# A decoder layer on one core: the order of three products at the opening of the mix

## The chip, the cores and the metric

The kernel runs on one core of a Trainium2 chip. The metric is the device time of one execution in microseconds (us); less is better. A core has five engines with a queue each: PE (matrix products, with its weight loads shown as PEld), DVE and POOL (elementwise work), ACT (elementwise functions and copies; it also issues DMAs) and SP (issues DMAs). Each engine takes the instructions of its queue in the order in which they were emitted.

## The reference

One layer of a hybrid decoder is computed for 1024 prompt tokens and 64 sample tokens (8 sequences of 8), 1088 in all, in float32:

```
h = x + 0.5 * swiglu(rmsnorm(x), ffn1)
n = rmsnorm(h)
proj = n @ w_in        # split into qkv_pre, z, a, b, q_s, k_s, v_s
qkv  = silu(causal_conv(qkv_pre))          # 12 tiles of 128 columns
g, beta = f(a), sigmoid(b)                 # a and b: 4 columns each, the "logits"
o_g  = gated_delta_chunked(qkv, g, beta)   # chunks of 64, a triangular solve per chunk, a state carried on
o_s  = sliding-window attention(q_s, k_s, v_s)
h = h + concat(o_g, o_s) @ w_out
h = h + 0.5 * swiglu(rmsnorm(h), ffn2)
h = h + sigmoid(rmsnorm(h) @ ple_gate) * (p @ ple_proj);  y = rmsnorm(h)
```

The middle part, from `n @ w_in` to the product with `w_out`, is called the mix.

## The kernel before, in words

Activations lie transposed, with 128 features on the partitions and the 1088 tokens along a row, and are worked on in four quarters of 272 columns (`QW`), numbered 0 to 3; quarters 0 and 1 are the first half, 2 and 3 the second. To keep float32 accuracy each operand is split into a high and a low part (`split`: ACT casts the high part, DVE or POOL subtracts to get the low one), and a product of one 128-column tile with one quarter is three products for each of 8 blocks of the inner dimension: 24 matmuls of 128x272, called a wide group here. In the trace they are `pm<-xn,t`.

The mix follows a hand-written list, `ORDER`: ('T', m) is the projection of tile m of `w_in`, ('co', m) its transposes back, ('sc',) the scalars from the logits, 'so' the triangular solves, 'lv' the levels that join solved blocks, 'pre', 'go' and 'out' the steps of the state, 'swa' the attention. A scheduler takes the program in this order and fixes each engine's queue, so that rows of neighbouring steps are interleaved on each engine.

The mix opens before the list is walked. Three products are cut into parts by quarter and their parts are collected in `joint`, by `logits()` and by `conv_in` for the first two tiles, 5 and 6:

- **the logits (L)**: 16 columns of weights for a and b. A group for one quarter is 16 matmuls, 8 with 16 and 8 with 8 columns of weights, on 272 columns (`pm<-xn,w`, form 16x272 and 8x272 in the order). The small weight tile w is loaded, cast on ACT and its low part taken on DVE (L207 `w<-raw,w`). Banks: pool g, two buffers.
- **tile 5 (A)**: four wide groups; those of quarters 0 and 1 go into one bank each of pools c and a, those of 2 and 3 into pool m, which has two buffers.
- **tile 6 (B)**: four wide groups, all in pool m.

All three use activations to which only the gain of the norm is applied; the root of each token is multiplied in when a group is evicted by DVE (`pre<-pm,r` for tiles, `abT<-pm,r` for the logits). For each half `mix_roots` forms the roots: sums on PE (`pss`), a chain of short DVE rows (`nv`, `nry`, `nrt`, `np`), diagonals on DVE and POOL (`dg`); `nm.sums` then spreads them with PE (`pb`) and copies them on ACT (`r<-pb`). No group of a half is evicted before that copy. The loop below counts the groups from n = 0 to 11, half by half: sums of the first half behind group 4, evictions from group 5 on, roots of the second half behind group 5, its sums behind group 7.

```
groups = [(half, part, 2 * half + i) for half in range(2) for part in parts_ for i in range(2)]
for n, (half, part, ci) in enumerate(groups):
    evs.append(part(ci))
    if n in (4, 7):
        nm.sums(half)
    if n >= 5 and n != 6:
        while evs:
            evs.pop(0)()
    if n == 5:
        mix_roots(1)
```

Behind the loop `lend()` transposes the logits (`pa<-ident,abT`) and stores them in `ab`. Then the list goes on: the short convolution of tile 5 (ACT L837, three DVE rows L839 over 1024 and three over 64 tokens, silu on ACT L840), its transposes (`ptk`), and the projection of the next tile, 4. The scalars (`ctmp`, `csg`) need `ab`; the decays of the chunks (`gu` on POOL, `pdc` on PE) need the scalars.

Of the kernel before, what the change touches and what calls it, by code (L numbers as in the profile page):

```python
# [150 lines left out]
def decoder_layer(ctx: ExitStack, tc: tile.TileContext, mix_off, a, o):  # L151
# [628 lines left out]
    joint = [None]  # L780
# [707 lines left out]
    ends = [conv_in(m, w) for m, w in zip(tiles[:2], ws)]  # L1488
    for e in ends:
        next(e)  # L1490
    parts_, joint[0] = joint[0], None
    def mix_roots(c):
        nm.roots(c, pt, "t", [B(b, [HW], "dg", F32R) for b in (14, 15)])

# [167 lines left out]
```

## Time and profile before

| | |
|---|---|
| median of three runs | 2326.74 us |
| the three runs | 2315.22, 2326.94, 2326.74 us |
| the profiled execution, its own time | 2301.93 us |
| its span, first to last instruction | 2300.1 us |
| PE busy in the span | 2234.6 us (97%) |
| DVE, ACT, POOL busy | 1424.9, 885.2, 528.8 us |
| mean granted clock of PE | 0.979 |

The profile is of one execution, which was 24.8 us shorter than the median of the three runs beside it; 1.8 us of its time lie outside the span. [...] Busy shares are means over stages: the first feed-forward part ends at about 768 us, the mix lies between there and about 1360 us, and the second feed-forward part and the gate fill the rest.

### The profile page before, as it was taken

The numbers are of one execution on the slowest core, as the hardware profiler recorded it, in microseconds if no ns is written. First come the engines' busy times: TensorE is split into PE (matmuls) and PEld (weight loads), VectorE is DVE, ScalarE is ACT, GpSimd is POOL, SyncE is SP. The second block draws the span as 40 slices with busy tenths as digits, with TensorE's granted clock in tenths as the row PEclk, the third lists the DMA queues.
The fourth block names the chain that finished last, engine by engine and source line by source line (L and its number), as shares of the span: only waits on it lengthen the run. The fifth ranks groups of instructions, "written<-read, shape, count | busy, mean of one in ns | idle before, by whom it ended". The sixth has DMA issues, their size and how long they took to land. (4 is left out here: it accounts for less than half of the span.)

```text
span 2300.1 us, 43650 instructions
## 1 busy us (share of the span) xinstructions
PE 2234.6 (97%) x17440; PEld 2181.6 (95%) x17440; DVE 1424.9 (62%) x2753; ACT 885.2 (38%) x1728; POOL 528.8 (23%) x448
## 2 busy tenths in 40 slices
PE   8999999999999999989999999999999999999997
PEld 8999999999999898889896789999999999999997
DVE  8866556975333477865654657866556684443667
ACT  6433333444322264322235654433333344332444
POOL 0043332210010334242321000333333210011324
PEclk9999999999999999988996999999999999999999
DMA  5322222367433245455552565222222258433234
GB/s 190 106 82 84 67 76 85 108 201 260 141 112 118 80 139 153 120 147 173 156 172 88 159 195 176 93 85 81 71 76 85 71 160 286 134 100 112 92 97 129
DMA packets 179354, 290.90 MB, mean 126 GB/s; under 512 B 33391, under 2 KB 87663, under 8 KB 179151
## 3 DMA queue, kind: packets, MB, share of 16 engines
q1 hardware_dynamic: 128288, 225.82, 32.2%
q10 hardware_dynamic: 50863, 62.29, 7.8%
q8 instruction: 137, 2.24, 0.4%
q14 instruction: 66, 0.54, 0.1%
HBM read 220.53 MB, written 66.83 MB: 125 GB/s over the span
## 5 line engine op out<-in xcount | busy, mean ns | idle before, releaser
L177 PE MATMUL pd<-xa,t 128*128 128x272 f32 x4224 | 531.8, 288 | 5.5 <-DVE s L463 3.8
L177 PEld LDWEIGHTS pd<-xa,t 128*128 128x128 f32 x4224 | 530.4, 188 | 6.8 <-DVE s L463 4.3
L177 PE MATMUL pm<-xn,t 128*128 128x272 f32 x2112 | 297.8, 297 | 15.0 <-DVE pre L824 7.2
L207 DVE TENSOR_TENSOR t<-raw,t 128x1024 fp32r<-128x1024 f32 x128 | 163.6, 1278 | 238.5 <-ACT t L206 235.8
L177 PEld LDWEIGHTS pm<-xn,t 128*128 128x128 f32 x2112 | 278.6, 194 | 21.3 <-DVE pre L824 8.5
L206 ACT CAST t<-raw 128x1024 fp32r<-128x1024 f32 x150 | 157.1, 1047 | 295.3 <-PE pd L177 226.8
L177 PE MATMUL pS<-lT,hS 128*128 128x272 f32 x900 | 260.4, 289 | 0.0
L177 PE MATMUL pS<-hT,lS 128*128 128x272 f32 x900 | 260.1, 289 | 0.0
L177 PE MATMUL pS<-hT,hS 128*128 128x272 f32 x900 | 259.1, 288 | 0.0
L207 DVE TENSOR_TENSOR lA<-raw,hA 128x512 fp32r<-128x512 f32 x171 | 136.9, 804 | 58.5 <-ACT hA L206 52.2
L177 PE MATMUL pA<-hB,lA 128*128 128x272 f32 x600 | 172.6, 288 | 0.0
L177 PE MATMUL pA<-hB,hA 128*128 128x272 f32 x600 | 172.5, 288 | 0.0
L177 PE MATMUL pA<-lB,hA 128*128 128x272 f32 x600 | 172.1, 287 | 0.0
L177 PEld LDWEIGHTS pS<-hT,hS 128*128 128x128 f32 x900 | 169.6, 188 | 0.0
L177 PEld LDWEIGHTS pS<-hT,lS 128*128 128x128 f32 x900 | 169.3, 188 | 0.0
L177 PEld LDWEIGHTS pS<-lT,hS 128*128 128x128 f32 x900 | 169.2, 188 | 0.0
L206 ACT CAST hA<-raw 128x512 fp32r<-128x512 f32 x171 | 105.8, 620 | 161.0 <-PE pA L177 121.6
L206 ACT CAST hS<-raw 128x512 fp32r<-128x512 f32 x145 | 89.4, 620 | 176.5 <-PE pS L177 154.2
L259 POOL TENSOR_TENSOR r<-r,sq 128x544 f32<-128x544 f32 x28 | 47.1, 1684 | 425.3 <-ACT sq L258 424.1
L207 DVE TENSOR_TENSOR lS<-raw,hS 128x512 fp32r<-128x512 f32 x145 | 127.8, 881 | 17.6 <-ACT hS L206 4.8
L463 DVE TENSOR_TENSOR u<-u,pS 128x272 f32<-128x272 f32 x225 | 91.1, 432 | 54.8 <-PE pS L177 54.6
L177 PEld LDWEIGHTS pA<-lB,hA 128*128 128x128 f32 x600 | 113.0, 188 | 0.0
(363 smaller groups left out, 4687.9 us busy)
## 6 DMA issues: line engine op xcount, KB each, us to landing
raw<-in_gu SPq DMA_DIRECT2D x114, 512.0 KB
raw<-in_dn SPq DMA_DIRECT2D x88, 512.0 KB
scrU<-act ACTq DMA_DIRECT2D x88, 272.0 KB
a<-scrU SPq DMA_DIRECT2D x88, 272.0 KB
raw<-in_gate SPq DMA_DIRECT2D x24, 512.0 KB
raw<-in_w_in SPq DMA_DIRECT2D x22, 512.0 KB
raw<-in_w_out SPq DMA_DIRECT2D x16, 512.0 KB
h<-in_x SPq DMA_DIRECT2D x2, 2176.0 KB
```

Source lines behind the costliest of these rows:

```text
L177: i = T.matmul(out, lhsT=lhsT, rhs=rhs, start=start, stop=stop)
L206: S.copy(hi, src)
L207: return eng.tensor_tensor(out=lo, in0=src, in1=hi.bitcast(F32), op=ALU.subtract)
L259: G.tensor_tensor(out=self.acc[c], in0=self.acc[c], in1=sq, op=ALU.add)
L463: i_ = V.tensor_tensor(out=I[c][out], in0=I[c][x], in1=pt_, op=ALU.add)
```

## The change

The list of collected parts is turned by one place, so that in each half the groups come as A, A, B, B, L, L in place of L, L, A, A, B, B. Nothing is computed otherwise; the numbers 4, 5, 6 and 7 in the loop stay, so the sums of the first half now stand behind the first logits group, those of the second behind tile 5's last group.

```
-    parts_, joint[0] = joint[0], None
+    parts_, joint[0] = joint[0][1:] + joint[0][:1], None
```

The queues are decided by the scheduler, which had already put wide groups ahead of the first logits. On PE at the opening, in the first half (`pss<-ones,r_6230` are the sums for its roots, `w_8999` is the weight tile of the logits; the logits' rows that follow alternate in the two forms):

```order
 L177 MATMUL pss<-ones,r_6230 128x2 x4
 L177 MATMUL pss<-ones,r_6230 32x2
-L177 MATMUL pm<-xn,t 128x272 x69
+L177 MATMUL pm<-xn,t 128x272 x96
 L177 MATMUL pm<-xn,w_8999 16x272
```

Before, 69 wide matmuls stood ahead of the first logits row (A's two groups and 21 rows of B's first); now 96 do, all four wide groups of the half. The numbers of rows in the opening are the same.

Further on, on DVE, in the convolution of tile 4 beside the projection of tile 7 (`pre<-pm,r_6230` are evictions of the projection, `cv` rows are the convolution):

```order
 L839 SCALAR_TENSOR_TENSOR cv<-pre,vecs,cv 128x1024
-L839 SCALAR_TENSOR_TENSOR cv<-pre,vecs,cv 128x64
 L824 TENSOR_TENSOR pre<-pm,r_6230 128x272
-L839 SCALAR_TENSOR_TENSOR cv<-pre,vecs,cv 128x1024
-L839 SCALAR_TENSOR_TENSOR cv<-pre,vecs,cv 128x64
-L839 SCALAR_TENSOR_TENSOR cv<-pre,vecs,cv 128x1024
+L839 SCALAR_TENSOR_TENSOR cv<-pre,vecs,cv 128x64
+L839 SCALAR_TENSOR_TENSOR cv<-pre,vecs,cv 128x1024
+L839 SCALAR_TENSOR_TENSOR cv<-pre,vecs,cv 128x64
 L824 TENSOR_TENSOR pre<-pm,r_6230 128x272
+L839 SCALAR_TENSOR_TENSOR cv<-pre,vecs,cv 128x1024
 L839 SCALAR_TENSOR_TENSOR cv<-pre,vecs,cv 128x64
```

Between the two evictions two long convolution rows stood before and one stands now.

In the levels, on DVE before (the first piece) and after (the second); `rot` is a tile that a DMA fills and POOL multiplies, `L1048` evicts the last product of the first two chunks:

```order
L1076 SCALAR_TENSOR_TENSOR X<-pkq,cssA,X 128x128 x4
L1030 TENSOR_TENSOR Pm<-plv,ctile 128x4x64 x3
L1048 TENSOR_SCALAR lv<-plv 64x4x64 x2
L1197 TENSOR_TENSOR xq<-xq,rope 128x1088
L1037 TENSOR_TENSOR lv<-lv,plv 128x8x32
```

```order
L1076 SCALAR_TENSOR_TENSOR X<-pkq,cssA,X 128x128 x4
L1030 TENSOR_TENSOR Pm<-plv,ctile 128x4x64 x3
L1197 TENSOR_TENSOR xq<-xq,rope 128x1088
L1048 TENSOR_SCALAR lv<-plv 64x4x64 x2
L1037 TENSOR_TENSOR lv<-lv,plv 128x8x32
```

The two evictions L1048 have moved behind the rotary row L1197; L1037 stands behind it in both.

In the attention, on ACT before (the first piece) and after (the second), behind the scaling of one attention unit (L1282); `sc<-px` copies transposed weights of the attention out of PSUM, `cvz` is the silu of a z tile:

```order
L1282 ACTIVATE sc<-sc,se 128x128 x2
L206 CAST t<-raw 128x1024
L1364 ACT_TABLE_LOAD
L1364 ACTIVATE cvz<-cvz 128x1088
L1287 COPY sc<-px 128x512
```

```order
L1282 ACTIVATE sc<-sc,se 128x128 x2
L1287 COPY sc<-px 128x2x128
L1287 COPY sc<-px 128x512
L206 CAST t<-raw 128x1024
L1262 ACTIVATE sc,den<-sc,nmx 128x256 x4
```

The copies have moved ahead of the cast, the table load and the silu.

## Rows read from the trace of the kernel before

**Rows 1.** The page: span, busy time of the engines.
```profile
span 2300.1 us, 43650 instructions
PE 2234.6 (97%) x17440; PEld 2181.6 (95%) x17440; DVE 1424.9 (62%) x2753; ACT 885.2 (38%) x1728; POOL 528.8 (23%) x448
```

**Rows 2.** Windows: stretch, length, busy time by engine, granted clock, DMA share, GB/s.
```profile
768.86:802.00 33.14, 30.02 (x233) 26.86 (x231) 18.72 (x56) 6.58 (x13) 11.55 (x14) 0.95 0.27 89
802.00:956.00 154.00, 148.39 (x1151) 143.78 (x1150) 116.31 (x252) 79.82 (x186) 58.65 (x68) 0.99 0.44 129
956.00:1013.00 57.00, 46.30 (x319) 45.14 (x318) 46.35 (x58) 15.96 (x47) 20.89 (x14) 0.88 0.59 159
1216.00:1248.00 32.00, 29.79 (x108) 21.02 (x109) 11.51 (x44) 16.77 (x49) 6.53 (x4) 0.52 0.40 132
1248.00:1300.00 52.00, 50.37 (x351) 36.66 (x352) 32.25 (x131) 33.79 (x113) 1.91 (x1) 0.93 0.39 119
```

**Rows 3.** Timeline of PE at the opening: start, length, row, [idle before, releaser].
```profile
768.86 8.91 PE L177 MATMUL pm<-xn,t 128*128 128x272 f32 x69
780.89 5.39 PE L177 MATMUL pm<-xn,w 128*16 128x272 f32 x32 [3.12 <-DVE w L207]
...
789.99 1.10 PE L177 MATMUL pss<-ones,r 128*128 128x2 f32 x10
791.02 4.13 PE L177 MATMUL pm<-xn,w 128*16 128x272 f32 x32
...
808.50 4.76 PE L177 MATMUL pm<-xn,t 128*128 128x272 f32 x36
```

**Rows 4.** Window around that idle time, columns as in rows 2.
```profile
780.00:784.00 4.00, 3.10 (x15) 1.94 (x16) 0.84 (x6) 0.06 (x1) 1.27 (x5) 0.57 0.92 298
```

**Rows 5.** Timeline of DVE at the opening.
```profile
780.66 0.18 DVE L207 TENSOR_TENSOR w<-raw,w 128x64 fp32r<-128x64 f32 x1
...
787.44 0.43 DVE L801 TENSOR_TENSOR abT<-pm,r 16x272 f32<-16x272 f32 x1 [6.60 <-ACT r L266]
```

**Rows 6.** Timeline of ACT at the opening.
```profile
783.94 0.21 ACT L892 ACTIVATE ctmp<-vecs 128x4 f32<-128x4 f32 x1 [4.37 <-POOL lmask L744]
786.95 0.68 ACT L266 COPY r<-pb 128x272 f32<-128x272 f32 x2 [2.81 <-PE pb L177]
```

**Rows 7.** Timelines of PE, DVE and POOL, and a window, 829 to 840 us.
```profile
829.15 3.25 PE L177 MATMUL pm<-xn,t 128*128 128x272 f32 x24
832.88 0.33 PE L177 MATMUL pdc<-gu,lmask 64*64 64x256 f32 x1 [0.48 <-POOL gu L948]
834.89 0.60 PE L177 MATMUL pm<-xn,t 128*128 128x272 f32 x1 [1.68 <-DVE pre L824]
...
829.01 3.35 DVE L839 SCALAR_TENSOR_TENSOR cv<-pre,vecs,cv 128x1024 f32<-128x1024 f32 x1
...
829.01 5.47 DVE L839 SCALAR_TENSOR_TENSOR cv<-pre,vecs,cv 128x1024 f32<-128x1024 f32 x3
834.41 0.43 DVE L824 TENSOR_TENSOR pre<-pm,r 128x272 f32<-128x272 f32 x1
...
828.89 2.39 POOL L207 TENSOR_TENSOR t<-raw,t 128x1024 fp32r<-128x1024 f32 x1
...
832.00:840.00 8.00, 5.84 (x34) 5.43 (x33) 3.98 (x7) 3.29 (x7) 1.92 (x4) 0.79 0.53 177
```

**Rows 8.** Timelines of ACT and PE in the attention.
```profile
1215.31 1.11 ACT L1364 ACTIVATE cvz<-cvz 128x1088 f32<-128x1088 f32 x1
1216.32 0.57 ACT L1287 COPY sc<-px 128x512 f32<-128x512 f32 x1
...
1217.22 1.55 PE L177 MATMUL po<-sc,vtok 128*64 128x128 f32 x12 [1.65 <-ACT sc L1287]
```

**Rows 9.** Timelines of PE and DVE in the levels, and a window.
```profile
1032.39 0.69 PE L1041 MATMUL plv<-ident,lv 128*128 128x128 f32 x4 [1.79 <-DVE lv L1037]
...
1030.72 1.29 DVE L1197 TENSOR_TENSOR xq<-xq,rope 128x1088 f32<-128x1088 f32 x1 [1.51 <-DMA rot<-xq]
...
1024.80:1057.40 32.60, 30.81 (x217) 29.75 (x216) 16.45 (x36) 3.36 (x12) 10.22 (x7) 0.74 0.72 207
```

## The prediction

> **What bounds the kernel now.** I read the page first. PE is busy for 2234.6 of 2300.1 us, so whatever moves the time must take idle time or slow time from PE; DVE, at 62%, can matter only where PE waits for it [rows 1]. The windows by stage come next, because a mean says nothing about the mix. In them the reader is to see that PE is close to full in most stretches, and that the losses are of two kinds: idle time (10.7 us of 57 between 956 and 1013 us, where DVE is busy for 46.35) and time at a lower granted clock (0.52 over the 32 us from 1216 us, which is the lower level for nearly all of it) [rows 2]. [...]
>
> Then the timeline of PE at the opening. 69 wide matmuls run from 768.86 to 777.77 us, which is 0.129 us each; then PE stands still for 3.12 us until 780.89, and the row says why: it waits for DVE's `w`, the low part of the logits' weights [rows 3]. That DVE row runs at 780.66 and takes 0.18, so w is there at 780.84 [rows 5]. The 32 logits matmuls behind the wait take 5.39 us, whereas the same 32 in the second half take 4.13 [rows 3]: 1.26 us more. The window agrees: granted 0.57 between 780 and 784 us is 1.72 us of lost clock, of which the 0.89 us before 780.89 was idle and cost nothing, which leaves about 1.3 [rows 4].
>
> **The change, part by part.**
>
> Opening. No row is added or removed; only the places differ. On PE the 27 wide matmuls that stood behind the first logits now stand ahead of them. At 0.129 us they take 3.5 us from 777.77, to 781.3, so w, there at 780.84, is no longer waited for, and PE does not pause. The saving is 3.12 us of idle time and, since the clock was full up to the pause, the 1.26 us behind it: 4.4 us. Its lower bound is nothing, if w comes later in the new queue; its upper bound is these 4.4, as the opening has no other wait of PE.
>
> What could take it back is the bank of the next wide group. Tile 5's third group now follows the logits at once and needs a buffer of pool m, so B's first group must have been evicted. From 781.3 PE still has two logits groups (4.13), four `pb` (0.5) and the sums of the second half (1.10), and arrives at 787.0. The copies of the root stand on ACT behind L892, which ends at 784.15; in the trace the first eviction starts 0.49 behind the start of those copies [rows 5, 6], so now at 784.6. Six evictions of 0.43 end by 787.2, and B's first is ahead of the last one, by 786.8. This I cost at nothing; the cover is 0.2 us at worst. If the copies are later still, each us is a us of PE.
>
> The second half's root chain starts some 4 us earlier with its sums. It has the two wide groups of tile 5 (48 matmuls, 6.2 us) and the logits behind it as cover, so nothing is waited for. The next tile's weights are cast when tile 5's last group ends; that group now ends earlier, with 4.1 us of logits and two wide groups behind it. Nothing there either. The scalars need the logits, which now end last, but two wide groups still follow them on PE, and everything of the scalars moves earlier with PE.
>
> Convolution beside tile 7. The scheduler's order changes here too. Before, PE ran 24 wide matmuls in 3.25 us, waited 0.48 for POOL's `gu` and 1.68 for an eviction. That eviction stood behind DVE rows that took 5.47 us together, of which the first long one took 3.35 [rows 7]. Now one long row stands between the two evictions in place of two: the other two rows of the three took 2.12, so the new distance is between about 2.4 us (a long row like the second and one more short row) and 3.9 (one like the first, and two short ones). PE's 24 matmuls cover 3.25. The wait is nothing at the lower end and 0.65 at the upper. The `pdc` product that waited 0.48 stands 48 wide matmuls (6.2 us) later against its partner, so its wait goes. The clock, 0.79 over the 8 us, lost 1.7 us of work [rows 7]. So the term lies between nothing (if the wait comes back as long elsewhere) and 0.48 + 1.68 + 1.7 = 3.9 us. I take 3.9, because the long row of 3.35 is the exception: the second one fitted in less than 2.12.
>
> [...] The long row of 3.35 us began 0.12 us after POOL's subtraction of 2.39 us [rows 7]. [...]
>
> Everything else. From 840 us on I move the rest of the program forward with these two terms. PE's and DVE's rows there depend on each other, not on a fixed clock time, and before 956 us DVE has 37.7 us of idle time in 154 [rows 2], so it can follow. The order differs in many other places, up to the end of the mix, and I cannot sum those; the two that stand out are rivals below.
>
> Sum: 4.4 + 3.9 = 8.3 us off the profiled execution's 2301.93, so 2293.6. That execution was 24.8 us below the median of the runs, and 8.3 us does not depend on which of them is meant; off the median of 2326.74 it gives 2318.4 us. A change of less than 0.5% (11.6 us) cannot be told from none here: the three runs alone span 11.7 us.
>
> **The rivals.**
>
> Much faster, by the attention. At 1217.22 PE waits 1.65 us for ACT's copies of `px`, which stand behind a cast, a table load and a silu of 1.11 us [rows 8]. In the changed order the copies stand ahead of all three, so that wait should go. The granted clock is 0.52 in the 32 us that follow, and 0.93 in the 52 us after, with the same kinds of rows at twice the rate [rows 2]. If the pause is what brought the clock down, up to 0.41 x 32 = 13.1 us go with it; together 14.8, and with my sum 2303.6 us. For it: the place is plain in both orders. Against it: in that stretch PE waits for others several times, and any of them may bring the clock down a few us later. By the rows the gain lies between 0 and 14.8; I leave it out of the sum, and let it draw the range downwards. Chance 0.27.
>
> Given back. Between 956 and 1013 us PE is idle for 10.7 us behind DVE's solve and convolutions [rows 2]. If DVE's chain does not start earlier, PE gets there 8.3 us sooner and waits 8.3 us longer: 2326.7. For it: DVE's 46.35 of 57. Against it: DVE's work before that depends on PE's rows, which are earlier. Chance 0.15.
>
> Slower, by the levels. The two evictions L1048 now stand behind the rotary row L1197, which in the trace idles 1.51 us for a DMA and takes 1.29 [rows 9]; they come up to 2.8 us later, and the joined blocks that they yield with them. PE, which already waits 1.79 us there, could wait 2.8 more. The clock is 0.74 over these 32.6 us [rows 9], 8.5 us of lost work; at the lower level throughout it would be 16.3. Price: 2.8 + 7.8 = 10.6, less my 8.3: 2329.0, slower than before. It decides from the point where this stretch loses 8.3 us. Against it: PE has other products to run there. Chance 0.10.
>
> The opening does not do what it says. If w comes more than 0.4 us later (781.3 less 780.84), PE pauses again; without the first term 2322.8. For it: w stands at the end of a long chain on DVE. Against it: nothing ahead of it on DVE has moved. Chance 0.06.
>
> **How the numbers follow.** My forecast has the remaining 0.42, with its own range of 2312 to 2323 (attention partly gained, second term partly lost). The predicted time is its 2318.4. The range of 2302 to 2331 takes in the attention rival nearly whole and the slower one, and leaves out less than 2 in 10. Faster by over 0.5% means below 2315.1: the attention rival and a third of the forecast, 0.27 + 0.13 = 0.40. Slower by over 0.5% means above 2338.4: only the slower rival with further waits of its kind, 0.05. Within 0.5%: 0.55.
>
> **What would show it.** In the changed profile: 96 wide matmuls without a pause, the first 32 logits matmuls as fast as the second (about 4.1 us), granted clock 1.00 from 776 to 790 us, and tile 4's projection starting at about 804.1 in place of 808.50 [rows 3]; no wait of over 0.7 us for `pre` between 820 and 840 us. For the attention rival, the granted clock of the stretch that answers to 1216 to 1248 us. The prediction is wrong if PE still waits for `w`, if tile 5's third group waits for an eviction, or if the 8.3 us are there at 840 us and gone at 1013.

## The result, and the profile after

The changed kernel is slower. Over twelve runs each, its median is 2323.31 us (2317.14 to 2327.48) and that of the kernel before 2312.86 us (2300.59 to 2327.40); the ratio is 1.0053, 95% interval 1.0027 to 1.0079, so about 12 us where I had forecast 8.3 us less. The three runs from which I took 2326.74 us were high draws of a kernel whose runs spread over 27 us. Ratios, here and below, leave out every run over 1.5% above the fastest of its kernel (two of e3, one of e10, two or three of before beside each experiment), so they are not the ratios of the medians shown.

The page of the changed kernel, first the span and the engines' busy time:

```profile
span 2321.5 us, 43639 instructions
PE 2257.4 (97%) x17440; PEld 2196.5 (95%) x17440; DVE 1425.9 (61%) x2753; ACT 883.9 (38%) x1728; POOL 523.5 (23%) x448
```

PE is busy for 22.8 us more than before with the same rows [rows 1]: it waits no longer, it runs slower. The mean granted clock, as a share of the full one, is 0.969 where before had 0.979; 2321.5 x 0.031 = 72 us of lost clock against 2300.1 x 0.021 = 48. The clock takes 24 us more and the span grew by 21.4, so all else together got 2 to 3 us shorter.

PE's timeline at the opening (start, length, row):

```profile
769.44 12.27 PE L177 MATMUL pm<-xn,t 128*128 128x272 f32 x96
781.55 2.16 PE L177 MATMUL pm<-xn,w 128*16 128x272 f32 x16
...
784.04 2.13 PE L177 MATMUL pm<-xn,w 128*16 128x272 f32 x16
786.00 1.10 PE L177 MATMUL pss<-ones,r 128*128 128x2 f32 x10
787.03 6.24 PE L177 MATMUL pm<-xn,t 128*128 128x272 f32 x48
...
804.60 1.28 PE L177 MATMUL pm<-xn,t 128*128 128x272 f32 x8
```

96 wide rows without a pause, no wait for `w`, the first 32 logits rows in 4.29 us in place of 5.39, tile 5's third group at once behind the sums at 787.03 and tile 4 at 804.60 in place of 808.50 [rows 3]. The opening does what it was forecast to do.

The windows of the changed kernel, columns as in rows 2:

```profile
768.86:802.00 33.14, 33.14 (x267) 30.76 (x267) 23.96 (x65) 10.90 (x18) 15.05 (x19) 1.00 0.33 110
802.00:956.00 154.00, 144.03 (x1129) 139.46 (x1128) 112.60 (x251) 76.06 (x182) 55.10 (x63) 1.00 0.46 135
956.00:1013.00 57.00, 52.01 (x392) 51.33 (x393) 46.70 (x59) 19.13 (x64) 22.08 (x15) 0.94 0.55 146
1216.00:1248.00 32.00, 30.18 (x118) 21.96 (x117) 14.47 (x43) 17.32 (x44) 5.87 (x4) 0.57 0.43 141
1248.00:1300.00 52.00, 50.51 (x194) 31.64 (x195) 22.81 (x96) 23.41 (x82) 1.91 (x1) 0.56 0.25 78
```

The reader is to see the fifth line. Between 1248 and 1300 us the granted clock was 0.93 [rows 2] and is 0.56; PE is as busy as before (50.5 of 52 us) and gets through 194 rows where it got through 351. The trace's record of the clock has two levels here, 1.00 and 0.50; the lower one holds for 47.8 us from 1254.1, where before it held for 6.8 us from 1254.7.

How far PE's rows stand ahead (-) or behind in us, found by matching the k-th row of each name and form in two traces and taking the median over a stretch, less the offset of the rows from 500 to 760 us. Stretches are by the kernel before; the last two columns are the experiments e10 and e3, below. Each column is one profiled execution:

```
stretch       changed     e10      e3
 800 to  820     -4.7    -4.7    -4.7
 840 to  870     -8.6    -8.6    -8.6
 900 to  930     -6.8    -7.9    -6.8
 985 to 1000     -4.1    -7.9    -3.8
1015 to 1030     -9.4    -7.9    -8.4
1060 to 1080     -6.0    -8.1    -4.2
1140 to 1160     -4.2    -7.2    -3.8
1250 to 1260     -5.8     2.4    -4.5
1280 to 1290     16.5     2.1     6.3
1300 to 1320     17.3     2.5    11.4
```

### The profile page after: what moved, and what is told of

Its sections match the earlier page's. It is cut to its first block, busy times and chain, and to the rows that moved or that the text cites. A ratio compares the mean times of both kernels' runs of the same rounds, so it can differ in the third digit from the quotient of the medians.

```text
span 2321.5 us, 43639 instructions
## 1 busy us (share of the span) xinstructions
PE 2257.4 (97%) x17440; PEld 2196.5 (95%) x17440; DVE 1425.9 (61%) x2753; ACT 883.9 (38%) x1728; POOL 523.5 (23%) x448
## 5 line engine op out<-in xcount | busy, mean ns | idle before, releaser
L463 DVE TENSOR_TENSOR u<-u,pS 128x272 f32<-128x272 f32 x225 | 91.1, 432 | 54.6 <-PE pS L177 54.3
```

Of the source, the lines that this page charges most:

```text
L463: i_ = V.tensor_tensor(out=I[c][out], in0=I[c][x], in1=pt_, op=ALU.add)
```

## The experiments

My theory (A in the expectations, then D) was that the changed order of the attention's rows holds the clock down behind 1250 us. The rivals: the moment at which the attention is reached (B), the middle of the mix (C), PE's busy share as what counts (E), the order of the other engines (F), and the order ahead of 1250 us (G, against H).

**How a queue is fixed.** Since the scheduler reorders everything behind the opening, the experiments join the queues of the two kernels: a table lists the rows of all engines in the wanted order, and each row is tied behind the one before it on its engine, by issue order alone.

```diff
+    want = np.cumsum(np.frombuffer(zlib.decompress(base64.b85decode(QUEUES)), np.int32))
+    rows = {i.name: i for i in nc.cur_bb.bb.instructions}
+    newest_on = {}
+    for k in want:
+        i = rows.get(f"I-{k}")
+        if i is not None:
+            e = str(i.engine)
+            if e in newest_on:
+                tc.add_manual_dep(i, newest_on[e], NOSYNC, reason="keeps the fixed queue")
+            newest_on[e] = i.name
```

The results together; the clocks of before are those of its 35 runs beside e1 to e4. Ratios are to the kernel before on the same chip, where its medians lay between 2309.58 and 2314.56 us, with 95% intervals; "clock" is the range of the mean clock over the runs; "low" is the time at the lower level in the profile, of the stretches that begin between 1245 and 1310 us.

| kernel | median us | ratio | clock | low, us |
|---|---|---|---|---|
| before | 2312.86 | | 0.962 to 0.982 | 6.8 |
| changed | 2323.31 | 1.0053 (1.0027 to 1.0079) | 0.967 to 0.971 | 47.8 |
| e1, queues of before | 2311.07 | 0.9986 (0.9953 to 1.0019) | 0.969 to 0.983 | 41.0 |
| e2, changed up to the opening's end | 2302.13 | 0.9968 (0.9933 to 1.0004) | 0.965 to 0.982 | 34.1 |
| e10, changed up to 868 us | 2305.06 | 0.9981 (0.9943 to 1.0018) | 0.961 to 0.981 | 6.8 |
| e3, changed up to the attention | 2310.09 | 0.9962 (0.9927 to 0.9998) | 0.964 to 0.981 | 44.4 |
| e4, changed from the attention on | 2329.42 | 1.0072 (1.0049 to 1.0095) | 0.966 to 0.973 | 54.6 |
| e11, changed up to 1250 us | 2311.01 | 1.0010 (0.9979 to 1.0041) | 0.970 to 0.978 | 27.3 |
| e12, changed but before from the attention to 1250 us | 2325.41 | 1.0046 (1.0009 to 1.0083) | 0.964 to 0.977 | 58.0 |
| e8, changed, PE regrouped | 2326.80 | 1.0057 (1.0029 to 1.0086) | 0.966 to 0.970 | 58.0 |
| e5, changed, three blocks of full rows | 2320.95 | 1.0033 (1.0003 to 1.0063) | 0.974 to 0.978 | 17.1 |
| e6, changed, three blocks of half rows | 2333.36 | 1.0100 (1.0067 to 1.0133) | 0.964 to 0.971 | 54.6 |
| e13, changed, one block of full rows | 2317.47 | 1.0023 (0.9990 to 1.0055) | 0.970 to 0.976 | 34.1 |
| e7, as e2, three blocks of full rows | 2302.09 | 0.9955 (0.9926 to 0.9983) | 0.976 to 0.983 | 13.7 |
| e9, as e10, five shorter blocks | 2303.77 | 0.9977 (0.9950 to 1.0003) | 0.976 to 0.982 | 6.8 |

**e1: the kernel before, its queues written out.**

> The kernel before, with each engine's queue written out row by row as the scheduler had it. Same time as before is expected by every theory. What it is for is its many runs with the clock of each: if the spread of the kernel before (2300.6 to 2327.4 us in twelve runs) is made by the granted clock of TensorE, time and mean clock go together, a run near 2301 has 0.979 as the profiled one had and a run near 2327 about 0.967, 2.3 us for each 0.001. If the spread is made by something else (transfers, the rows before 768 us), the clock stays within 0.002 while the time moves by 27 us.

Time and clock go together over twelve runs: 2297.02 us at 0.983, 2310.08 at 0.977, 2323.77 at 0.969, which is 1.9 us for each 0.001. So the spread of the kernel before goes with the clock. In the profile of this run the lower level held for 34.1 us from 1274.4, where the profile of before had the full level: the same queues give both.

**e2, e3 and e4: the change cut in parts.** Nothing but the table differs; e2 joins behind the last eviction of the logits, e3 and e4 ahead of the attention's first row.

> The queues of the changed kernel up to the last eviction of the logits, those of the kernel before from there on: the opening's change alone. Theory A (the order of the rows that the scheduler made in the attention keeps the clock low there and costs 20 us): the opening gives its 4.4 us and nothing takes it back, so the profile is near 2297, the clock 0.979 or more, and the median about 4 us below before. Theory B (any kernel that arrives at the attention at another moment may find the clock low; the order has nothing to do with it): a median anywhere between 2297 and 2323, with a clock between 0.967 and 0.981. Theory C (the middle of the mix, 870 to 1200 us, takes back what the opening gave): PE's rows at 1190 us are about where they were before, within 1 us, and the time is that of before.

> The queues of the changed kernel up to the first row of the attention, those of the kernel before from there on. Theory A (the attention's order costs the 20 us): time near the fast runs of before, 2299 to 2303 in the profile, with the clock at its lower level for less than 15 us between 1250 and 1305 us, and a median at least 8 us below the changed kernel's 2323. Theory B (the moment of arrival, not the order): as the changed kernel, near 2320, since the arrival at the attention is the changed kernel's.

> The queues of the kernel before up to the first row of the attention, those of the changed kernel from there on. Theory A (the attention's order): the lower level holds for over 40 us between 1250 and 1305 us, clock 0.967 to 0.971, time 2320 to 2327 in nearly all runs, as the changed kernel. Theory B (the moment of arrival): spread and median of the kernel before, 2300 to 2327 with a median near 2313.

e3 holds all of the change but the attention's order. Its ratio is 0.38% below before, 8.8 us, with an interval from 0.02% to 0.73%; the medians of all runs, 2310.09 and 2313.73, are only 3.6 us apart. e4 holds nothing of the change but the attention's order and is 0.72% slower, 17 us. Theory A holds for e4's clock, which is 0.966 to 0.973 in all twelve runs; in time most of them lie above the 2320 to 2327 us that I had expected. Theory B holds in part: with the order of before, e2 and e3 find the clock anywhere between 0.964 and 0.982, as before does. I had expected less than 15 us at the lower level in e3's profile; it had 44.4. Theory C does not hold: from 1180 to 1200 us PE's rows in e2 stand at -7.9 us. The order of before leaves it open whether the clock falls; the changed order, in the twelve runs each of e4 and of the changed kernel, does not.

The clock is not all of it. I laid a straight line through the runs of before beside each experiment, time against mean clock; it falls by 2.0 to 2.1 us for each 0.001. At the same clock the runs of e2, e3 and e10 lie 4.9 to 5.3 us below that line on the mean (standard errors 0.4 to 0.8), which is about the idle time in my sum, 3.12 + 0.48 + 1.68 = 5.3. Those of e4 lie 6.7 us above it (0.6). e4's mean clock, 0.970 against 0.974 of before, is worth some 8 us more. The pages of e1 and then of e4 agree: PE is idle for 66.2 us in e1 and for 72.0 in e4.

```profile
span 2316.1 us, 43650 instructions
PE 2249.9 (97%) x17440; PEld 2194.4 (95%) x17440; DVE 1424.9 (62%) x2753; ACT 884.1 (38%) x1728; POOL 528.0 (23%) x448
```

```profile
span 2329.1 us, 43647 instructions
PE 2257.1 (97%) x17440; PEld 2195.5 (94%) x17440; DVE 1426.3 (61%) x2753; ACT 883.9 (38%) x1728; POOL 528.2 (23%) x448
```

**e10: the changed queues up to 868 us.**

> The queues of the changed kernel up to 868 us (the opening and the convolution beside tile 7), those of the kernel before from there on. My two terms, 4.4 and 3.9 us, are both in it. If the order of the changed kernel between 868 and 1165 us is what gave 4 us back (its rows stood at -8.0 us at 870 and at -3.6 at 1160), PE's rows here stand 8 to 9 us ahead of before at 870 and still at 1160, and the median is about 8 us below before. If DVE's chain gives it back whatever the order, they stand at about -4 at 1160 and the median is that of before less 3 to 4 us.

PE's rows stand at -8.6 us at 870 and still at -7.2 at 1160, where e3, with the changed order in between, is back at -3.8 (table above). So in these two profiles 3.4 us are given back between 868 and 1165 us where the order is the changed one, and DVE does not take them back by itself. They are time at the lower level of the clock: in the levels, from about 1020 to 1065 us, it held for 23.9 us in e3 and for 17.1 in e10, but for 30.7 in e1, which has the order of before. That the order is what gives them back is therefore not shown. The ratio is 0.19% below before, and the interval takes in both nothing and the forecast 8.3 us: single runs go from 2290.9 to 2336.0 with the clock.

**e5 and e6: blocks of full and of half rows.** Twenty extra rows ahead of the po rows of three attention units; e6 has `[:64]` for `[:128]`.

```diff
         po = bank("po", [2, P], "po")
+        for _ in range(20 if (g, u) in ((1, 1), (0, 0), (0, 1)) else 0): T.matmul(po, lhsT=ones_r[:128], rhs=bc(ones_r[:128], 1, 2), start=True, stop=True)
         for q in range(2):
```

> The queues of the changed kernel, and in three attention units (those whose po rows ran at 1257, 1267 and 1284 us in the changed profile) 20 extra rows of ones by ones, 128x256 over all 128 partitions, into the bank that po is about to fill; the output is unchanged. A row of 128x272 took 0.129 us at full clock, so the 60 rows cost 7.3 us if the clock is up and 14.6 us if it stays down. Theory D (in this stretch the clock stays down because most rows use only 64 of the 128 partitions; full rows in a block bring it back): the clock rises within a few us of the first block, the 47.8 us at the lower level shrink to under 20 us, mean clock 0.975 or more, time about 2323 + 7 - 14 = 2316 us. Rival E (the clock looks at PE's busy share, which is 97% here already; extra rows change nothing): the lower level holds through, clock 0.966 to 0.970, time 2323 + 14.6 = 2338 us.

> The same 60 extra rows at the same places, 128x256, but over 64 of the 128 partitions: the same columns, hence the same length at the same clock. Theory D: they do not bring the clock back, the lower level holds from about 1255 us for over 50 us, clock at 0.966 to 0.970, time about 2323 + 14.6 = 2338 us, 20 us above the kernel with full rows. Rival E (any busy row counts alike): this kernel and the one with full rows have the same time and the same clock within 4 us and 0.002.

Windows of e5, and then of e6, columns as in rows 2:

```profile
1250.00:1264.00 14.00, 13.38 (x76) 10.43 (x75) 5.84 (x27) 7.48 (x26) 0.00 (x0) 0.78 0.06 17
1264.00:1286.00 22.00, 20.18 (x130) 14.15 (x128) 11.48 (x42) 9.97 (x38) 1.91 (x1) 1.00 0.44 133
```

```profile
1250.00:1264.00 14.00, 12.45 (x73) 9.34 (x74) 7.16 (x34) 8.80 (x33) 0.00 (x0) 0.85 0.09 29
1264.00:1286.00 22.00, 22.00 (x79) 15.32 (x78) 5.56 (x25) 7.61 (x28) 1.91 (x1) 0.50 0.28 88
```

PE's timeline in e5 at the first two blocks, and in e6 at the second:

```profile
1252.76 4.14 PE L1290 MATMUL po<-ones 128*128 128x256 f32 x20
1256.83 1.09 PE L177 MATMUL po<-sc,vtok 128*64 128x128 f32 x16
...
1262.39 2.64 PE L1290 MATMUL po<-ones 128*128 128x256 f32 x20
```

```profile
1264.68 4.63 PE L1290 MATMUL po<-ones 64*128 64x256 f32 x20
1269.25 0.69 PE L177 MATMUL po<-sc,vtok 128*64 128x128 f32 x4
```

In e5 the first block begins at the lower level, which ends at 1256.2 by the record of the clock, and behind it the 16 po rows take 1.09 us, full speed; the second block, at 1262.39, finds the full level and takes 2.64 us. In e6 a block of the same columns at the lower level (0.23 us a row) leaves the clock where it was: 4 po rows take 0.69 us, and the second window is at 0.50 with PE busy for all of its 22 us. That is e6's second block, and the third is like it; the first is not. Five of its rows started between rows of pr, the lower level ended at 1256.3, and the 16 po rows behind it ran at full speed:

```profile
1256.40 1.95 PE L1290 MATMUL po<-ones 64*128 64x256 f32 x15
1258.28 1.09 PE L177 MATMUL po<-sc,vtok 128*64 128x128 f32 x16
```

So the blocks taken one by one do not decide between D and E. The runs do: over ten runs each no clock of e5 is below 0.974 and none of e6 above 0.971, and the height of the extra rows is all that differs. That is as theory D had it, and shown for these two kernels alone. In time e5 won only 2 us on the changed kernel by the medians, 5 by the ratios, not 7: with the clock up, PE waits for other engines (1.8 us of the 22).

**e13: one block.** The same line with `((1, 1),)`.

> The queues of the changed kernel with a single block of 20 extra full rows (ones by ones, 128x256, 128 partitions) ahead of the po rows that ran at 1257 us; they cost 2.4 us at full clock. With three such blocks the clock was down for 17 us between 1249 and 1300 in place of 47.8. If the lower level keeps itself (few full rows pass while PE runs at half speed, so that one lift is enough), the clock rises once near 1260 us and stays for 20 us or more: clock 0.974 or more in most runs, median near 2323 + 2.4 - 14 = 2311 us. If the changed order lets it fall at once again: clock 0.967 to 0.972, median 2321 to 2326 us.

The lift came, and did not last to the end. PE's timeline:

```profile
1256.63 3.92 PE L1290 MATMUL po<-ones 128*128 128x256 f32 x20
1260.48 1.09 PE L177 MATMUL po<-sc,vtok 128*64 128x128 f32 x16
...
1271.99 0.92 PE L177 MATMUL pr<-ksT,sc 64*128 64x128 f32 x4
...
1274.57 2.07 PE L177 MATMUL pr<-ksT,sc 64*128 64x256 f32 x4
```

Full level from 1259.5 to 1273.2, where no wait of PE stands, then the lower one for 27.3 us. The median of 2317.47 lies between the two expectations.

**e8: regrouping without extra rows.** Ten rows of PE as emitted change places (not 14, as the expectation has it); the first of four places in its queue:

```diff
+L177 MATMUL pr<-ksT,sc 128x256 x2
 L1286 MATMUL px<-ident,sc 128x128 x8
-L177 MATMUL pr<-ksT,sc 128x256 x2
 L177 MATMUL po<-sc,vtok 64x128 x8
```

> The queues of the changed kernel with nothing added: on PE alone, 14 rows of the attention between 1250 and 1290 us change places, so that the rows over 128 partitions (px, po) stand in blocks as the kernel before has them and the rows over 64 partitions (pr, pSs) stand ahead of or behind the block. Theory D (rows over 128 partitions in a block bring the clock back, and the changed order had cut the blocks): the time at the lower level behind 1250 us shrinks from 47.8 to under 25 us in the profile, mean clock 0.973 or more in most runs, median 2308 to 2315 us. Rival F (it is the order of the other engines, or the moment, and the grouping on PE is nothing): clock 0.967 to 0.971 and 2317 to 2327 us in all runs, as the changed kernel.

Theory D failed here as I had put it: the clock was down for 58.0 us, and 0.966 to 0.970 in all runs, about as rival F has it. PE's timeline says what I had not counted:

```profile
1253.34 2.07 PE L177 MATMUL pr<-ksT,sc 64*128 64x256 f32 x4 [0.99 <-DVE mx L1256]
1255.34 1.97 PE L1286 MATMUL px<-ident,sc 128*128 128x128 f32 x8
1258.04 1.98 PE L177 MATMUL po<-sc,vtok 128*64 128x128 f32 x16 [0.74 <-ACT sc L1287]
```

The pr rows had stood between px and po as cover for ACT's copy. Without them the block has a gap of 0.74 us in it, and pr, now earlier, waits for its bank.

**e11 and e12: the attention cut at 1250 us.**

> The queues of the changed kernel up to the po rows at 1250 us, those of the kernel before from there on. Theory H (it is the order of the rows behind 1250 us that leaves the clock down): at least a third of the runs have a clock of 0.975 or more and stand below 2312 us, as in the kernels that keep the attention of before. Theory G (it is the order ahead of 1250 us, which sets how the stretch is entered): 0.967 to 0.972 in all runs, 2315 to 2328 us, as in the changed kernel.

> The queues of the changed kernel up to the first row of the attention, those of the kernel before up to the po rows at 1250 us, and those of the changed kernel behind. Theory H: the clock stays between 0.964 and 0.972 in all runs and the time above 2315 us. Theory G: at least a third of the runs have 0.975 or more and stand below 2312 us.

The part behind 1250 us carries most of it: with the order of before there, the changed kernel's time falls from 1.0053 to 1.0010 of before; with the order of before only ahead of it, 1.0046 is left, and seven of twelve runs lie above 2324 us. Neither theory has its numbers whole: only one run of e11 reaches 0.975 where I had expected a third, and two of e12 do where H had none. PE's timeline of e11 shows how the clock came back there:

```profile
1252.15 1.97 PE L1286 MATMUL px<-ident,sc 128*128 128x128 f32 x8
1254.05 1.98 PE L177 MATMUL po<-sc,vtok 128*64 128x128 f32 x16
1255.96 0.69 PE L177 MATMUL pvs<-kv,X 64*64 64x128 f32 x2
1256.57 0.43 PE L177 MATMUL pvs<-ident,kq 128*64 128x128 f32 x2
```

px and po stand together without a gap, and the record of the clock rises at 1256.5. In the changed kernel four rows of pr stand between them (next section) and the lower level stays.

**e7 and e9: the opening with blocks.**

> The opening's change alone (queues of the kernel before from the end of the opening on), with the 60 extra full rows in the same three attention units. Its twin without these rows ran at 2293.9 to 2327.6 us with clocks of 0.965 to 0.982. Theory D: the clock between 1250 and 1310 us is at its full level nearly throughout in every run, so the spread shrinks: all runs between 2297 and 2308 us, none above 2312, clock 0.979 to 0.984. Rival E: the spread stays, 2301 to 2335 us, clock down to 0.965 in some.

> As the kernel with the queues of the changed one up to 868 us, with 10 extra rows of ones by ones (128x256, 128 partitions) ahead of the po rows in five attention units. The 50 rows cost 6 us at full clock. Theory D: the clock stays up in most of the stretch between 1215 and 1310 us in every run, mean clock 0.980 or more, all runs within about 12 us of each other, median near 2298, which is below both kernels. Rival E: the spread of before (30 us) stays and the rows only cost: median near 2310.

The blocks narrow the spread, as theory D has it: e2's runs lie between 2293.9 and 2327.6 us, e7's between 2297.9 and 2315.9, with no clock below 0.976. Not by as much as I had expected: three runs of e7 lie above 2312 us where D had none, and e9's span 20 us, not 12. The medians of e2 and e7 are the same; what the clock gives, the extra rows and PE's waits take. e7 is the one kernel of the study whose interval stays well clear of before, 0.45% faster (0.17 to 0.74), and it is below the changed kernel by more.

## Why the prediction was wrong

**Opening: right.** 4.4 us forecast, 4.2 to 4.7 measured in e2, e3, e10 and the changed kernel. The two covers that I costed at nothing cost nothing. The 1.26 us of the clock in it were there in the profiled execution and not in every one: in e1, behind a wait of the same length, the 32 logits rows took 4.14 us in place of 5.39. So no run shows that the 1.26 us here, or the 1.7 of clock in the next term, were made by the waits ahead of them.

```profile
781.30 4.14 PE L177 MATMUL pm<-xn,w 128*16 128x272 f32 x32 [3.12 <-DVE w L207]
```

**Convolution beside tile 7: right, at the upper end.** 3.9 us forecast, and 3.9 measured (from -4.7 to -8.6). PE and DVE there:

```profile
821.77 3.48 PE L177 MATMUL pm<-xn,t 128*128 128x272 f32 x26
825.09 0.63 PE L177 MATMUL pdc<-gu,lmask 128*128 128x512 f32 x2
825.56 5.65 PE L177 MATMUL pm<-xn,t 128*128 128x272 f32 x44
...
822.06 2.91 DVE L839 SCALAR_TENSOR_TENSOR cv<-pre,vecs,cv 128x1024 f32<-128x1024 f32 x1 [2.39 <-ACT cv L837]
824.89 0.43 DVE L824 TENSOR_TENSOR pre<-pm,r 128x272 f32<-128x272 f32 x1
...
821.49 2.40 POOL L207 TENSOR_TENSOR t<-raw,t 128x1024 fp32r<-128x1024 f32 x1
```

No row of PE waits, and the granted clock is 1.00 from 820 to 840 us, where it was 0.79 from 832 to 840 before [rows 7]. The long DVE row took 2.91 us beside POOL's subtraction of 2.40 and ended 1.08 us behind its end; the one of 3.35 us before also ended 1.08 us behind the end of the subtraction beside it [rows 7]. That the one holds up the other is not shown by these two rows. In the changed kernel the wait of up to 0.65 us that I had set as the upper end did not come. e2, with the order of before there, gained 2.4 of the 3.9 us too, so the changed order is not alone in the term.

**"I move the rest of the program forward with these two terms": wrong by half up to 1165 us in the changed profile.** 8.6 us ahead at 870 became 4.2 at 1160. The rival "given back" had its place right and did not last: at 1000 us the rows stood at -4.1, at 1020 at -9.4. The rival "slower, by the levels" happened as described at 3.4 of its 10.6 us (-9.4 to -6.0). PE and DVE there:

```profile
1022.58 1.97 PE L177 MATMUL plv<-lv,AT 128*128 128x64 f32 x8 [1.67 <-DVE lv L1048]
...
1020.91 1.29 DVE L1197 TENSOR_TENSOR xq<-xq,rope 128x1088 f32<-128x1088 f32 x1 [1.64 <-DMA rot<-xq]
1022.12 0.74 DVE L1048 TENSOR_SCALAR lv<-plv 64x256 f32<-64x256 f32 x2
```

L1048 stands behind the rotary row that waits for its DMA, and PE waits for L1048, at the lower level of the clock for 23.9 us where before had 17.1. The 6.8 us more at half speed are the 3.4 us; as e1 had 30.7 us there with L1048 in its old place, that the new place did it is not shown.

**The step that failed** is the one that sets the attention aside: "By the rows the gain lies between 0 and 14.8; I leave it out of the sum, and let it draw the range downwards." The place was right and the lower bound was not. PE's timeline in the attention:

```profile
1213.70 0.88 PE L177 MATMUL po<-sc,vtok 128*64 128x128 f32 x12
...
1220.11 1.97 PE L1286 MATMUL px<-ident,sc 128*128 128x128 f32 x8 [1.41 <-ACT sc L1282]
...
1252.54 1.13 PE L177 MATMUL pr<-ksT,sc 64*128 64x256 f32 x4 [0.85 <-DVE mx L1256]
1253.60 1.51 PE L1286 MATMUL px<-ident,sc 128*128 128x128 f32 x8
1255.05 2.07 PE L177 MATMUL pr<-ksT,sc 64*128 64x256 f32 x4
1257.05 1.97 PE L177 MATMUL po<-sc,vtok 128*64 128x128 f32 x16
1258.95 0.69 PE L177 MATMUL pvs<-kv,X 64*64 64x128 f32 x2
```

ACT there:

```profile
1216.57 1.28 ACT L1364 ACT_TABLE_LOAD   x1
1217.86 1.11 ACT L1364 ACTIVATE cvz<-cvz 128x1088 f32<-128x1088 f32 x1
...
1219.55 0.90 ACT L1282 ACTIVATE sc<-sc,se 128x256 f32<-128x256 f32 x2
```

The wait for ACT's copies is gone, as the order said (po begins at 1213.70 with no wait). ACT's table load and silu then stand ahead of its next scaling, PE waits 1.41 us for that at 1220.11, and the clock falls at 1220.0 all the same: 0.57 over the 32 us where I had hoped for 0.93. What I had not priced at all is the stretch behind. I took its 0.93 as its own. It had 0.43 x 52 = 22 us to lose, more than twice my whole sum, and lost 0.37 x 52 = 19. That the profiled execution took 24.8 us less than the median shown was on the table: between the profiles of before and of e1, which have the same queues, the clock of this stretch differs most, and I set the difference aside as a matter of no consequence. That 2323.31 us lies within my range of 2302 to 2331 is luck: the base of 2326.74 was 13.9 us above the median of twelve runs, and the kernel moved the other way.

**What is shown and what is not.** That the attention's order costs 17 to 21 us by the ratios (e4; the changed kernel against e3) and some 15 by the means of all runs of e4 is shown, and that most of it comes from the order behind 1250 us (e11, e12). The clock between 1250 and 1305 us carries more than half of it (windows, clocks of e4, e5 and e6); about 7 us of e4's remain at the same mean clock, and of these only the idle time in its profile is known. That the cut between px and po is what holds the clock down is argued from e11 and the changed kernel; e8, which should have shown it, put a gap there, and e12 ran at both levels. The order of the other engines (F) changes with PE's in e4, e11 and e12, and e8, the one kernel that reordered PE's rows alone, went as F had it. Both stay open, as does why runs of the same queues differ.

## What to carry to other kernels

When a profiled execution is much faster than the runs beside it, find the stretch where they can differ before pricing a change, and price every stretch at full clock as one that can drop, as the 52 us from 1248 us did here from 0.93 to 0.56: its loss at the lower level is a bound of the range. A scheduler that decides the queues makes an edit at one end a new order at the other; fix the queues with a table, join old and new at a few points, and the parts can be timed apart. Where a good edit is spoilt by what the scheduler does later, keep the edit and the old order behind it.

## What the runs showed of the hardware

PE was busy by the profile for 50.5 of the 52 us from 1248 us in the changed kernel, with the clock at the lower level for 47.8 us from 1254.1; in e6 it was busy for all of the 22 us from 1264, at 0.50 throughout. In these stretches busy time by the profile did not tell the level.

Within twenty rows of 256 columns over 128 partitions that began at the lower level the full one came back: at 1256.2 in e5, in a block from 1252.76 to 1256.90, and at 1259.5 in e13, in a block from 1256.63 to 1260.55. With twenty over 64 partitions it did not at two of the three places in e6, where the twenty took 4.63 us each time, and at the first it did, at 1256.3. Over ten runs each the mean clocks are 0.974 to 0.978 with the full rows and 0.964 to 0.971 with the half rows.

At the full level the twenty full rows took 2.64 us in e5, which is 0.132 us a row; at the lower one the twenty half rows of e6 took 4.63 us, 0.23 a row.
